# The first shift and scale with the modulation matrix as the stationary operand, for all eight output tiles

## The chip, the cores and the metric

The kernel runs on one core of a Trainium2 chip. The metric is the device time of one execution in microseconds (us); the median of three runs of the kernel before is 1396.38 us, the runs lie between 1396.1 and 1402.08. The engines are named as in the profile: PE multiplies matrices, PEld is PE's loading of the stationary operand, DVE, ACT and POOL work on vectors, SP and ACT issue the transfers (DMA).

## The reference

Two transformer blocks on a sequence of 256 tokens (stream x) beside a context of 256 tokens (stream ctx), model width 1024. What matters here is the beginning of the first layer: a modulation vector is made for each stream from its condition vector, and the first two of its six parts shift and scale the normalised activations ahead of the first projection.

```python
sc, scc = jax.nn.silu(c), jax.nn.silu(c_ctx)
mod   = jnp.split(sc  @ w_mod[l] + b_mod[l], 6, axis=-1)   # shift1, scale1, gate1, ...
mod_c = jnp.split(scc @ w_mod[l] + b_mod[l], 6)
hn = rms_norm(h, g_norm1[l]) * (1 + mod_c[1]) + mod_c[0]
xn = rms_norm(x, g_norm1[l]) * (1 + scale1) + shift1
pc, p = hn @ w_in[l], xn @ w_in[l]
```

After that come attention, a Fourier mixer, a convolution and a pooling mixer on slices of p, the output projection and a gated feed-forward, for two layers, and then a second block of the same kind. All of it is float32.

## The kernel before

Activations lie with the features on the 128 partitions: XC holds 8 tiles (k = 0 to 7) of 128 features by 512 columns, 256 of stream x and 256 of the context. Large products are made with three matmuls each (`mm3`, lines 273 to 275) from a rounded high part and a rest: AH and AL of the activations, wh and wl of the weights. The weights come as 512 KB halves through a ring of four raw buffers, are cast to wh by ACT (line 243) and reduced to wl by DVE (line 245; the second half by POOL). SP issues the transfers in the order in which the code names them; the other engines' instructions are put in order by a scheduler when the kernel is built, and each engine then works through its own list in that order.

The first projection, p_c, takes four output tiles of `in0` and accumulates over the eight k in four PSUM banks: 12 matmuls of 512 columns for each k. Before tile k can be multiplied its scale and shift must be known: `modv[:, 0, 1, :, k]` and `modv[:, 0, 0, :, k]`, two numbers for each feature, one for each stream. They are made in two ways:

- k = 0 to 3: `scf` (silu of the two condition vectors, 128 x 2 for each of eight input tiles) is the stationary operand and 512 columns of the matrix `rawm` are the moving one (line 431, p_mod, 16 matmuls). The result has two rows; ACT copies them out (line 456), PE turns them by transposes (line 459, p_modt), DVE adds the bias and forms the scale (lines 464 and 466).
- k = 4 to 7: the function `st_tile` loads one output tile of the matrix (wms, 512 KB, with the outputs on the partitions) for the scale and one for the shift. DVE multiplies it by `scb[:, 0]` and sums along the row (line 494), POOL multiplies it by `scb[:, 1]` (line 493) and ACT sums that (line 496); DVE adds the bias (lines 499 and 501). `scb` holds the condition vectors spread over all partitions; 16 transposes (line 372, p_scb) and four copies make it at the very start.

The function `in0_k` then normalises tile k (lines 481 to 485) and issues its 12 matmuls. `rb`, the reciprocal root of the mean square spread over partitions, comes from squares (lines 309 to 315), 8 matmuls with one column (line 440, p_ss), a DVE and a POOL step (lines 298 and 299) and four transposes (line 444, p_rb). After p_c come p_q, the query projection (lines 289 to 291), and p_cv, the first taps of the convolution (line 578). `scb` is also used much later by `mod_bg`, which makes the other parts of the modulation in the background.

Of the kernel before, what the change touches and what calls it, by code (L numbers as in the profile page):

```python
# [24 lines left out]
F32 = mybir.dt.float32  # L25
F32R = mybir.dt.float32r
I32 = mybir.dt.int32
AF = mybir.ActivationFunctionType
OP = mybir.AluOpType
AX = mybir.AxisListType  # L30

D = 1024
KT = 8
# [7 lines left out]
UW = T + 2 * POOL_PAD  # L41

RAW, WB, EV, NT, PTB, PEB, WMB = 4, 4, 4, 2, 2, 2, 4
WRB, WSB, N0B = 4, 5, 2
KP = 4
XAT = (0, 1, 1, 2)
RWP, XR0 = 0, 2
NPE = 8
CVD, FOD = 0.9, 1
BG0, BG1 = 2.4, 2.0  # L50
# [104 lines left out]
def tile_kernel(ctx, tc, xin, pk_d, rows_d, lc_d, bc_d, wmod0, wmod, win, wout, wfi, wfo, wsm, win2, wproj, wout2,  # L155
                wgu, wdn, wst, pos, out, dump=None):
    nc = tc.nc
    V, S, G, PE, SP = nc.vector, nc.scalar, nc.gpsimd, nc.tensor, nc.sync
# [4 lines left out]
    cpool = ctx.enter_context(tc.tile_pool(name="cp", bufs=1))  # L163
    ring = ctx.enter_context(tc.tile_pool(name="ring", bufs=1))
    wk = ctx.enter_context(tc.tile_pool(name="wk", bufs=2))
    psum = ctx.enter_context(tc.tile_pool(name="ps", bufs=4, space=bass.MemoryType.PSUM))

    def pmm(name="pmm"):
        return psum.tile([128, 512], F32, tag="mm", name=name)

    def psm(name="psm"):
        return psum.tile([128, 512], F32, tag="sm", name=name)
# [52 lines left out]
    ld = {"lim": 10 ** 6, "dma": 0, "split": 0, "raw": {}, "hl": {}}  # L225

    def dma_to(i):
        while ld["dma"] < min(i, len(halves), ld["lim"]):
            j = ld["dma"]
            raw = ring.tile([128, 1024], F32, tag="raw", name="raw", bufs=RAW)  # L230
            SP.dma_start(raw[:, :halves[j][1]], halves[j][0])
            ld["raw"][j] = raw
            ld["dma"] += 1

    def split_to(i):
        while ld["split"] < min(i, len(halves)):
# [12 lines left out]
            dma_to(j + 1 + RAW)
# [111 lines left out]
    modv = cpool.tile([128, 2, 6, 2, KT], F32, name="modv")  # L361
    scf = cpool.tile([128, KT, 2], F32, name="scf")
    for s in range(2):
        S.activation(scf[:, :, s], P("c", 8 * s, 8), AF.Silu)
    scb = lpool.tile([128, 2, D], F32, name="scb")
    lc = lpool.tile([128, LC_W], F32, name="lc")

    for s in range(2):
        for a in range(2):
            p = psm("p_scb")  # L370
            for k in range(4):
                PE.transpose(p[:, 128 * k:128 * k + 128], scf[:, 4 * a + k, s:s + 1].to_broadcast([128, 128]), ident)
            (S.copy if a else V.tensor_copy)(scb[:, s, 512 * a:512 * a + 512], p)

    def mv(l, part, s):
        return modv[:, l, part, s]
# [39 lines left out]

    sctx = ctx.enter_context(ExitStack())
    spool = sctx.enter_context(tc.tile_pool(name="st", bufs=1))
    nj = KP // 2
    ps = [pmm("p_mod") for _ in range(nj)]  # L420
    raws = []
    for k in range(KT):
        raw = spool.tile([128, 256 * KP], F32, tag="wr", name="rawm", bufs=WRB)
        raws.append(raw)
        SP.dma_start(raw, wmod0[k])
        for i, at in enumerate(XAT):
            if at == k:
                SP.dma_start(XC[:, 2 * i:2 * i + 2], xin[:, 2 * i:2 * i + 2])
    for k in range(KT):
        for j in range(nj):  # L430
            PE.matmul(ps[j][:2], scf[:, k, :], raws[k][:, 512 * j:512 * j + 512], start=k == 0, stop=k == KT - 1)
    new_ss(True)
    for k in range(KT):
        sq_acc(k, slice(0, 512), k == 0, V)
    dma_to(2)
    ld["lim"] = 2
    p = psm("p_ss")
    for i in range(4):
        for n, ss in enumerate(ss_t["ss"]):
# [2 lines left out]
    rb = psm("p_rb")  # L442
    for i in range(4):
        PE.transpose(rb[:, 128 * i:128 * i + 128], r[:, i:i + 1].to_broadcast([128, 128]), ident)
    bm1 = cpool.tile([128, KT], F32, name="bm1")
    V.tensor_scalar(bm1, P("bmod0", 8, 8), 1.0, None, op0=OP.add)
    xr = [None] * KT
    for k in range(0, XR0, 2):
        x2 = spool.tile([128, 2, 512], F32, tag="wr", name="xr", bufs=WRB)
        for i in range(2):  # L450
            V.tensor_tensor(x2[:, i], XC[:, k + i], rb, op=OP.mult)
            xr[k + i] = x2[:, i]
    pt = psm("p_modt")
    for j in range(nj):
        row = wk.tile([128, 512], F32, tag="ev", name="row", bufs=EV)
        S.copy(row[:2], ps[j][:2])
        for b in range(4):
            o = 2 * (4 * j + b)
            PE.transpose(pt[:, o:o + 2], row[:2, 128 * b:128 * b + 128], ident[:2, :2])
    ptv = pt[:, :4 * KP].rearrange("p (a k s) -> p a k s", a=2, s=2)  # L460
    for part in (1, 0):
        for s in range(2):
            d = modv[:, 0, part, s, 0:KP]
            V.tensor_tensor(d, ptv[:, part, :, s], P("bmod0", part * 8, KP), op=OP.add)
            if part == 1:
                V.scalar_tensor_tensor(d, d, 1.0, P("g1_0", 0, KP), op0=OP.add, op1=OP.mult)
    n_ = "in0"
    ps4 = [pmm("p_c") for _ in range(4)]

    def in0_k(k):  # L470
        t = spool.tile([128, 512], F32, tag="n0", name="n0", bufs=N0B)
        if xr[k] is None and k % 2 == 0:
            x2 = spool.tile([128, 2, 512], F32, tag="wr", name="xr", bufs=WRB)
            xr[k], xr[k + 1] = x2[:, 0], x2[:, 1]
        for s in (0, 1):
            c = slice(256 * s, 256 * s + 256)
            if k < XR0:
                S.activation(t[:, c], xr[k][:, c], AF.Identity, bias=mv(0, 0, s)[:, k:k + 1],
                             scale=mv(0, 1, s)[:, k:k + 1])
            else:  # L480
                V.scalar_tensor_tensor(xr[k][:, c], XC[:, k, c], mv(0, 1, s)[:, k:k + 1], rb[:, c], op0=OP.mult,
                                       op1=OP.mult)
                S.activation(t[:, c], xr[k][:, c], AF.Identity, bias=mv(0, 0, s)[:, k:k + 1])
        S.copy(AH[:, k, 0:512], t)
        V.tensor_tensor(AL[:, k, 0:512], t, AH[:, k, 0:512].bitcast(F32), op=OP.subtract)
        for m in range(4):
            mm3(ps4[m], wk256(n_, m // 2, k, 128 * (m % 2)), act(k, slice(0, 512)), k == 0, k == KT - 1)

    def st_tile(part, k):
        w = spool.tile([128, D], F32, tag="wms", name="wms", bufs=WSB)  # L490
        SP.dma_start(w, wmod[0, 8 * part + k])
        jg = spool.tile([128, D], F32, tag="jgs", name="jgs", bufs=2)
        G.tensor_tensor(jg, w, scb[:, 1], op=OP.mult)
        V.scalar_tensor_tensor(w, w, 1.0, scb[:, 0], op0=OP.mult, op1=OP.mult,
                               accum_out=modv[:, 0, part, 0, k:k + 1])
        S.activation(jg, jg, AF.Copy, accum_out=modv[:, 0, part, 1, k:k + 1])
        d = modv[:, 0, part, :, k]
        if part == 1:
            V.tensor_scalar(d, d, bm1[:, k:k + 1], P("g1_0", k), op0=OP.add, op1=OP.mult)
        else:  # L500
            V.tensor_scalar(d, d, P("bmod0", k), None, op0=OP.add)

    split_to(2)
    for i in range(2 * (KT - KP)):
        if i == RWP:
            ld["lim"] = WB
            split_to(WB)
        st_tile(1 - i % 2, KP + i // 2)
    ld["lim"] = 10 ** 6
    SP.dma_start(rows, bass.AP(tensor=rows_d.tensor, offset=rows_d.offset, ap=[[0, 128], [1, 512]]))  # L510
    SP.dma_start(lc, lc_d)
    dma_to(WB + RAW)
    for k in range(KT):
        in0_k(k)
    sctx.close()


# [2 lines left out]
    for l in range(2):  # L520
# [4 lines left out]
        with ExitStack() as mctx:  # L525
# [319 lines left out]
            for s in streams[::-1]:  # L845
                for i in range(2):
                    p = pmm("p_q")
# [550 lines left out]
def _pack(inp):  # L1398
    inp = {k: np.asarray(v) for k, v in inp.items()}
    a = {}  # L1400
# [25 lines left out]
    rows += [inp["sgu_ln_g_2"][0], inp["sgu_ln_b_2"][0]]  # L1426
    a["rows"] = np.concatenate(rows)
    a["lc"], a["bc"] = _shape_consts()
    a["wmod0"] = inp["w_mod"][0][:, :2048].reshape(8, 128, 2, 1024)[..., :128 * KP].reshape(8, 128, 256 * KP)
    a["wmod"] = inp["w_mod"].transpose(0, 2, 1).reshape(2, 48, 128, 1024)  # L1430
    qcols = np.concatenate([h * 64 + dh for h in (0, 2, 1, 3)])
    kcols = 256 + np.concatenate([h * 64 + dh for h in (0, 1)])
# [53 lines left out]
```

## Time and profile before

| | us |
|---|---|
| median of three runs | 1396.38 |
| lowest and highest run | 1396.1, 1402.08 |
| the profiled execution | 1395.62 |
| its span, first to last instruction | 1393.4 |
| mean granted PE clock | 0.983 of full |
| p_c over, p_q begins | 74.8, 75.5 |

The profile is one execution. PE is busy 1339.7 us of the span, DVE 932.3, ACT 617.5, POOL 287.9. [...] A matmul's row has its start and a modelled end; what one costs in a row of equal ones is read from the distance of two starts. A float32 matmul that is not a transpose stands in the trace as two records (two passes), each with its own weight load, and an `mm3` matmul as one.

### The profile page before, as it was taken

Reading aid. Unit: us, or ns where it says so; the run is one execution under the profiler, and the core shown is the slowest. Engines: PE = TensorE matmul, PEld = TensorE weight load, DVE = VectorE, ACT = ScalarE, POOL = GpSimd, SP = SyncE. Lnnn points to the kernel's source line nnn. Section 1 sums busy time; section 2 is a strip of 40 time slices with the busy share of each in tenths; the row PEclk is TensorE's granted clock in tenths of the full one; section 3 lists DMA queues with packets and bytes.
Section 4 is the critical chain, followed back from the end, with each engine's and each line's share of the span. In section 5 each row is a group of like instructions: output and inputs, shape, how many; then the busy total and the mean of one; then the engine's idle time right before and its main releaser. Section 6 shows DMA issues by size and latency. Waiting matters only on the chain.

```text
span 1393.4 us, 23072 instructions
## 1 busy us (share of the span) xinstructions
PE 1339.7 (96%) x9000; PEld 1193.2 (86%) x9000; DVE 932.3 (67%) x1597; ACT 617.5 (44%) x1030; POOL 287.9 (21%) x302
## 2 busy tenths in 40 slices
PE   6799889999999999999899999999999999999997
PEld 2578558888888888889689999999899999999997
DVE  4969999899885333349757666666665567755553
ACT  5623452523214232334555554455665444544452
POOL 3524535233340000121520000120100002322211
PEclk9799989999999999999999999999999999999998
DMA  8322443477895222343225555665325335555463
GB/s 321 136 92 79 166 154 134 152 272 232 278 323 179 91 91 63 104 137 107 78 83 189 183 182 156 187 242 191 122 98 175 122 125 179 181 182 181 153 196 106
DMA packets 66477, 223.77 MB, mean 161 GB/s; under 512 B 7488, under 2 KB 8640, under 8 KB 66368
## 3 DMA queue, kind: packets, MB, share of 16 engines
q1 hardware_dynamic: 53824, 178.16, 38.3%
q10 hardware_dynamic: 12080, 42.50, 9.0%
q0 software_dynamic: 464, 1.64, 0.3%
q8 instruction: 70, 1.15, 0.3%
q14 instruction: 39, 0.32, 0.1%
HBM read 221.22 MB, written 1.05 MB: 160 GB/s over the span
## 4 chain that ended last, share of the span: by engine, by line
PE 84%; DVE 9%; issue 2%; DMA 2%; POOL 1%; ACT 1%; SPq 0%; DVEq 0%; POOLq 0%; ACTq 0%
PE p_dn L273 6%; PE p_dn L275 6%; PE p_dn L274 6%; PE p_ua L273 4%; PE p_ua L274 4%; PE p_ug L273 4%; PE p_ug L275 4%; PE p_ug L274 4%; PE p_ua L275 4%; DVE wm L404 2%; DVE jg L402 2%; PE p_bq L289 2%; PE p_bq L290 2%; PE p_bq L291 2%; PE p_ga L275 2%
## 5 line engine op out<-in xcount | busy, mean ns | idle before, releaser
L245 DVE TENSOR_TENSOR wl<-raw,wh 128x1024 fp32r<-128x1024 f32 (+2 forms) x340 | 390.5, 1151 | 277.7 <-ACT wh L243 275.7
L243 ACT CAST wh<-raw 128x1024 fp32r<-128x1024 f32 (+1 forms) x344 | 331.6, 972 | 310.0 <-PE p_ug L274 89.2
L275 PE MATMUL p_dn<-HH,wl 128*128 128x256 f32 (+1 forms) x550 | 171.9, 313 | 0.5 <-DVE wl L245 0.5
L273 PE MATMUL p_dn<-HH,wh 128*128 128x256 f32 (+1 forms) x550 | 172.0, 313 | 0.0
L274 PE MATMUL p_dn<-HL,wh 128*128 128x256 f32 (+1 forms) x550 | 171.9, 312 | 0.0
L315 POOL TENSOR_TENSOR ss<-ss,sq 128x256 f32<-128x256 f32 (+1 forms) x43 | 49.8, 1158 | 422.2 <-ACT sq L314 284.7
L273 PE MATMUL p_ug<-AH,wh 128*128 128x258 f32 (+2 forms) x368 | 121.9, 332 | 0.6 <-DVE XC L891 0.6
L273 PE MATMUL p_ua<-AH,wh 128*128 128x258 f32 (+2 forms) x368 | 122.0, 333 | 0.4 <-ACT usg L950 0.3
L275 PE MATMUL p_ug<-AH,wl 128*128 128x258 f32 (+2 forms) x368 | 122.0, 332 | 0.0
L274 PE MATMUL p_ug<-AL,wh 128*128 128x258 f32 (+2 forms) x368 | 121.9, 331 | 0.0
L274 PE MATMUL p_ua<-AL,wh 128*128 128x258 f32 (+2 forms) x368 | 121.9, 331 | 0.0
L275 PE MATMUL p_ua<-AH,wl 128*128 128x258 f32 (+2 forms) x368 | 121.7, 331 | 0.0
L275 PEld LDWEIGHTS p_dn<-HH,wl 128*128 128x128 f32 x550 | 104.4, 190 | 6.7 <-DVE wl L245 0.7
L273 PEld LDWEIGHTS p_dn<-HH,wh 128*128 128x128 f32 x550 | 104.4, 190 | 6.1 <-ACT wh L243 0.2
L274 PEld LDWEIGHTS p_dn<-HL,wh 128*128 128x128 f32 x550 | 104.4, 190 | 6.1
L404 DVE SCALAR_TENSOR_TENSOR wm<-wm,scb 128x1024 f32<-128x1024 f32 x80 | 100.9, 1265 | 11.2 <-DMA wm<-in_wmod 10.4
L273 PEld LDWEIGHTS p_ug<-AH,wh 128*128 128x128 f32 x368 | 69.3, 188 | 8.1 <-DVE XC L891 0.8
L273 PEld LDWEIGHTS p_ua<-AH,wh 128*128 128x128 f32 x368 | 69.2, 188 | 7.7 <-ACT usg L950 0.5
L274 PEld LDWEIGHTS p_ua<-AL,wh 128*128 128x128 f32 x368 | 69.4, 189 | 7.3 <-DVE AL L341 0.2
L275 PEld LDWEIGHTS p_ua<-AH,wl 128*128 128x128 f32 x368 | 69.4, 189 | 7.1
L274 PEld LDWEIGHTS p_ug<-AL,wh 128*128 128x128 f32 x368 | 69.5, 189 | 6.9
L275 PEld LDWEIGHTS p_ug<-AH,wl 128*128 128x128 f32 x368 | 69.4, 189 | 6.9
(375 smaller groups left out, 3415.5 us busy)
## 6 DMA issues: line engine op xcount, KB each, us to landing
raw<-in_wfi SPq DMA_DIRECT2D x88, 512.0 KB, 4.0
raw<-in_win SPq DMA_DIRECT2D x84, 512.0 KB, 4.0
wm<-in_wmod ACTq DMA_DIRECT2D x80, 512.0 KB, 4.4
raw<-in_wgu SPq DMA_DIRECT2D x44, 512.0 KB, 3.8
raw<-in_wout SPq DMA_DIRECT2D x24, 512.0 KB, 3.6
raw<-in_wfo SPq DMA_DIRECT2D x32, 384.0 KB, 3.1
raw<-in_wfo SPq DMA_DIRECT2D x32, 320.0 KB, 3.3
raw<-in_wdn SPq DMA_DIRECT2D x16, 384.0 KB, 3.1
```

The costliest lines, as they stand in the source:

```text
L243: S.copy(h[:, :n], raw[:, :n])
L245: (G if every and j % every == 0 else V).tensor_tensor(lo[:, :n], raw[:, :n], h[:, :n].bitcast(F32), op=OP.subtract)
L273: PE.matmul(ps, w[0], a[0], start=first, stop=False, **kw)
L274: PE.matmul(ps, w[0], a[1], start=False, stop=False, **kw)
L275: PE.matmul(ps, w[1], a[0], start=False, stop=last, **kw)
L289: PE.matmul(ps, a[0], w[0], start=k == 0, stop=False)
L290: PE.matmul(ps, a[0], w[1], start=False, stop=False)
L291: PE.matmul(ps, a[1], w[0], start=False, stop=k == KT - 1)
L315: (eng or G).tensor_tensor(ss[0][:, cs], ss[0][:, cs], sq[:, :n], op=OP.add)
L402: V.scalar_tensor_tensor(jg, w, 1.0, scb[:, 1], op0=OP.mult, op1=OP.mult, accum_out=modv[:, l, part, 1, k:k + 1])
L404: V.scalar_tensor_tensor(w, w, 1.0, scb[:, 0], op0=OP.mult, op1=OP.mult, accum_out=modv[:, l, part, 0, k:k + 1])
```

## The change

All sixteen output tiles of the matrix (scale and shift, k = 0 to 7) are loaded as wms tiles, in a new layout: the inputs on the partitions, the 128 outputs along the row. For each tile k the new function `mod_k` issues 2 x 8 matmuls with a 128 x 128 piece of wms as the stationary operand and the two columns of `scf` as the moving one; the result has the outputs on the partitions, and two DVE instructions finish it. The helpers `in0_k`, `st_tile`, the transposes p_modt and the row copies are gone, as is POOL's and ACT's part in the modulation; the normalisation uses the function `norm_k` of the later layers (tiles of 256 columns). XC is loaded ahead of the matrix. `mod_k(k + 1)` is written ahead of tile k's part of p_c. The filling of `scb` is written behind p_c.

```diff
-RAW, WB, ... = 4, 4, ...
-WRB, WSB, N0B = 4, 5, 2
-KP = 4
-XAT = (0, 1, 1, 2)
-RWP, XR0 = 0, 2
+WSB = 9
+RWP = (2, 6)
...
+    def scb_fill():
...  (the p_scb transposes and copies, unchanged)
...
+    for i in range(4):
+        SP.dma_start(XC[:, 2 * i:2 * i + 2], xin[:, 2 * i:2 * i + 2])
+    wms = {}
+    ld["lim"] = 0
     for k in range(KT):
-        raw = spool.tile([128, 256 * KP], F32, tag="wr", name="rawm", bufs=WRB)
-        raws.append(raw)
-        SP.dma_start(raw, wmod0[k])
...
-    for k in range(KT):
-        for j in range(nj):
-            PE.matmul(ps[j][:2], scf[:, k, :], raws[k][:, 512 * j:512 * j + 512], start=k == 0, stop=k == KT - 1)
+        if k in RWP:
+            ld["lim"] += 2
+            dma_to(ld["lim"])
+        for part in (1, 0):
+            wms[part, k] = spool.tile([128, D], F32, tag="wms", name="wms", bufs=WSB)
+            SP.dma_start(wms[part, k], wmod0[8 * part + k])
+    ld["lim"] = 10 ** 6
+    SP.dma_start(rows, ...)
+    SP.dma_start(lc, lc_d)
...
+    def mod_k(k):
+        p = psm("p_mod")
+        for part in (1, 0):
+            for j in range(KT):
+                PE.matmul(p[:, 2 * part:2 * part + 2], wms[part, k][:, 128 * j:128 * j + 128], scf[:, j, :],
+                          start=j == 0, stop=j == KT - 1)
+        V.tensor_scalar(modv[:, 0, 1, :, k], p[:, 2:4], bm1[:, k:k + 1], P("g1_0", k), op0=OP.add, op1=OP.mult)
+        V.tensor_scalar(modv[:, 0, 0, :, k], p[:, 0:2], P("bmod0", k), None, op0=OP.add)
...
-    pt = psm("p_modt")
...
-    def in0_k(k):
...
-    def st_tile(part, k):
-        w = spool.tile([128, D], F32, tag="wms", name="wms", bufs=WSB)
-        SP.dma_start(w, wmod[0, 8 * part + k])
-        jg = spool.tile([128, D], F32, tag="jgs", name="jgs", bufs=2)
-        G.tensor_tensor(jg, w, scb[:, 1], op=OP.mult)
-        V.scalar_tensor_tensor(w, w, 1.0, scb[:, 0], op0=OP.mult, op1=OP.mult,
-                               accum_out=modv[:, 0, part, 0, k:k + 1])
-        S.activation(jg, jg, AF.Copy, accum_out=modv[:, 0, part, 1, k:k + 1])
...
+    mod_k(0)
+    split_to(2)
     n_ = "in0"
     ps4 = [pmm("p_c") for _ in range(4)]
+    for k in range(KT):
+        if k + 1 < KT:
+            mod_k(k + 1)
+        if k == 2:
+            split_to(WB)
         for s in (0, 1):
...
+            norm_k(s, k, mv(0, 1, s), mv(0, 0, s), rb[:, 256 * s:256 * s + 256])
         for m in range(4):
             mm3(ps4[m], wk256(n_, m // 2, k, 128 * (m % 2)), act(k, slice(0, 512)), k == 0, k == KT - 1)
...
+    scb_fill()
     sctx.close()
```

PE's list at the start of the program, the kernel before: the transposes p_scb come first, p_mod has 512 moving columns, and p_ss and p_rb lie between its parts.

```order
L372 MATMUL p_scb<-ident,scf 128x128 x16
L431 MATMUL p_mod<-rawm,scf 2x512 x6
L440 MATMUL p_ss<-ones,ss 128x1
...
L431 MATMUL p_mod<-rawm,scf 2x512 x6
L444 MATMUL p_rb<-ident,rs_r 128x128 x4
L431 MATMUL p_mod<-rawm,scf 2x512 x2
L459 MATMUL p_modt<-ident,row 128x2 x8
L273 MATMUL p_c<-AH,wh 128x512 x4
L274 MATMUL p_c<-AL,wh 128x512
```

The same place of the changed kernel, where p_mod has two moving columns and each matmul listed makes two passes in the trace:

```order
L451 MATMUL p_ss<-ones,ss 128x1
L451 MATMUL p_ss<-ones,ssl 128x1
...
L455 MATMUL p_rb<-ident,rs_r 128x128 x4
L440 MATMUL p_mod<-scf,wms 128x2 x32
L271 MATMUL p_c<-AH,wh 128x512
L272 MATMUL p_c<-AL,wh 128x512
L273 MATMUL p_c<-AH,wl 128x512
...
L440 MATMUL p_mod<-scf,wms 128x2 x16
...
L372 MATMUL p_scb<-ident,scf 128x128 x12
L271 MATMUL p_c<-AH,wh 128x512
...
L372 MATMUL p_scb<-ident,scf 128x128 x4
L287 MATMUL p_q<-wh,AH 128x256
```

PE begins with p_ss, the modulation of tiles 0 and 1 stands behind p_rb, that of tile k + 2 behind tile k's part of p_c, and p_scb has moved to both sides of tile 7's part.

SP's list of transfers at the start, the kernel before (rawm and wms are the modulation matrix, raw the weights of the first projection):

```order
L425 DMA rawm<-in_wmod 128x1024
L428 DMA XC<-in_xin 128x1024
...
L428 DMA XC<-in_xin 128x1024 x2
L425 DMA rawm<-in_wmod 128x1024
L428 DMA XC<-in_xin 128x1024
L425 DMA rawm<-in_wmod 128x1024 x5
L231 DMA raw<-in_win 128x1024 x4
L491 DMA wms<-in_wmod 128x1024 x8
L510 DMA rows<-in_rows 128x512
```

The same place of the changed kernel:

```order
L420 DMA XC<-in_xin 128x1024 x4
L429 DMA wms<-in_wmod 128x1024 x4
L229 DMA raw<-in_win 128x1024 x2
L429 DMA wms<-in_wmod 128x1024 x8
L229 DMA raw<-in_win 128x1024 x2
L429 DMA wms<-in_wmod 128x1024 x4
L431 DMA rows<-in_rows 128x512
```

XC has moved ahead of the matrix; the number of 512 KB tiles is the same, 4 of XC, 16 of the matrix, 4 of weights.

## Rows read from the trace of the kernel before

**Rows 1.** The page: the chain that ended last, shares of the span.

```profile
PE 84%; DVE 9%; issue 2%; DMA 2%; POOL 1%; ACT 1%; SPq 0%; DVEq 0%; POOLq 0%; ACTq 0%
```

**Rows 2.** Stretches: us, busy us of PE, PEld, DVE, ACT, POOL, then PEclk, DMA.

```profile
0.00:30.00 30.00, 21.43 (x76) 8.47 (x76) 11.12 (x22) 16.54 (x35) 5.77 (x10) 1.00 0.91 331
30.00:75.00 45.00, 29.88 (x96) 22.02 (x96) 39.43 (x50) 23.39 (x44) 25.42 (x20) 0.77 0.45 155
```

**Rows 3.** Groups by form, 30 to 68 us, p_c's to 75: busy, mean ns, idle before.

```profile
L493 POOL TENSOR_TENSOR jgs<-wms,scb 128x1024 f32<-128x1024 f32 x8 | 24.0, 3018 | 7.4 <-ACT jgs L496 6.9 <-DMA wms<-in_wmod 0.5
L494 DVE SCALAR_TENSOR_TENSOR wms<-wms,scb 128x1024 f32<-128x1024 f32 x8 | 11.9, 1493 | 0.0
L274 PE MATMUL p_c<-AL,wh 128*128 128x512 f32 x32 | 15.9, 495 | 6.9 <-DVE AL L485 6.9
L273 PE MATMUL p_c<-AH,wh 128*128 128x512 f32 x32 | 10.7, 462 | 9.9 <-ACT AH L484 9.9
```

**Rows 4.** PE in order of time, p_c: start, duration, what, count.

```profile
69.38 0.63 PE L275 MATMUL p_c<-AH,wl 128*128 128x512 f32 x1
69.80 0.63 PE L274 MATMUL p_c<-AL,wh 128*128 128x512 f32 x1
...
74.42 0.40 PE L274 MATMUL p_c<-AL,wh 128*128 128x512 f32 x1
74.66 0.39 PE L275 MATMUL p_c<-AH,wl 128*128 128x512 f32 x1
```

**Rows 5.** The chain that ended last, in order of time: start, us, what.

```profile
4.31 9.36 DMA XC<-in_xin
```

**Rows 6.** ACT, DVE and POOL in order of time: start, duration, what, count.

```profile
3.77 4.78 ACT L570 ACTIVATE cdg<-ident,pk 128x128 f32<-128x128 f32 x16 [0.67 <-POOL pk L197]
...
11.09 3.08 DVE L315 TENSOR_TENSOR ss<-ss,sq 128x512 f32<-128x512 f32 x4 [0.31 <-ACT sq L314]
...
19.35 1.04 POOL L299 TENSOR_TENSOR rs_r<-rs_v,mhalf 128x4 f32<-128x4 f32 x1 [15.62 <-DVE rs_v L298]
```

**Rows 7.** PE in order of time: the transposes p_scb and p_rb, and p_ss.

```profile
3.14 3.65 PE L372 MATMUL p_scb<-ident,scf 128*128 128x128 f32 x16 [3.14 <-ACT scf L364]
...
17.59 0.36 PE L440 MATMUL p_ss<-ones,ss 128*128 128x1 f32 x2
...
18.70 0.36 PE L440 MATMUL p_ss<-ones,ssl 128*128 128x1 f32 x2
...
24.24 0.65 PE L444 MATMUL p_rb<-ident,rs_r 128*128 128x128 f32 x4
```

**Rows 8.** Weight loads of p_c by form, 49.0 to 54.4 us, then 41.2 to 44.3.

```profile
L274 PEld LDWEIGHTS p_c<-AL,wh 128*128 128x128 f32 x5 | 1.7, 330 | 0.5
...
L274 PEld LDWEIGHTS p_c<-AL,wh 128*128 128x128 f32 x4 | 0.8, 189 | 0.2
```

**Rows 9.** PE in order of time at 188 us: p_var with one moving column.

```profile
188.14 1.95 PE L611 MATMUL p_var<-ones,lsq 128*128 128x1 f32 x16 [0.44 <-DVE awo L737]
190.01 1.12 PE L689 MATMUL p_s<-KTt,QT 64*128 64x512 f32 x2
```

**Rows 10.** Stretches around p_var (columns as in Rows 2).

```profile
188.00:190.00 2.00, 1.86 (x16) 1.86 (x16) 2.00 (x4) 1.19 (x4) 0.65 (x1) 1.00 0.72 223
190.00:192.00 2.00, 2.00 (x7) 0.94 (x6) 2.00 (x7) 0.93 (x3) 1.02 (x2) 0.80 0.55 160
192.00:194.00 2.00, 2.00 (x11) 1.30 (x12) 2.00 (x5) 0.62 (x2) 1.63 (x2) 0.50 0.60 207
```

**Rows 11.** PE in order of time: p_c begins again after two waits.

```profile
48.65 0.79 PE L274 MATMUL p_c<-AL,wh 128*128 128x512 f32 x1 [3.19 <-DVE AL L485]
...
68.78 0.79 PE L274 MATMUL p_c<-AL,wh 128*128 128x512 f32 x1 [1.63 <-DVE AL L485]
```

**Rows 12.** The stretches in which PEclk rises after them (columns as in Rows 2).

```profile
54.00:56.00 2.00, 2.00 (x9) 1.65 (x8) 2.00 (x3) 1.97 (x4) 2.00 (x1) 0.84 1.03 388
...
70.00:72.00 2.00, 2.00 (x7) 1.58 (x6) 0.46 (x1) 0.00 (x0) 1.40 (x9) 0.57 0.26 49
```

More of the change, by code (lines that the diff above doesn't have):

```diff
@@ L366, in tile_kernel @@
     lc = lpool.tile([128, LC_W], F32, name="lc")
[L368 to L373, printed above, removed]
+    def scb_fill():
+        for s in range(2):
+            for a in range(2):
+                p = psm("p_scb")
+                for k in range(4):
+                    PE.transpose(p[:, 128 * k:128 * k + 128], scf[:, 4 * a + k, s:s + 1].to_broadcast([128, 128]), ident)
+                (S.copy if a else V.tensor_copy)(scb[:, s, 512 * a:512 * a + 512], p)
     def mv(l, part, s):
@@ L418, in tile_kernel @@
     spool = sctx.enter_context(tc.tile_pool(name="st", bufs=1))
-    nj = KP // 2
-    ps = [pmm("p_mod") for _ in range(nj)]
-    raws = []
+    for i in range(4):
+        SP.dma_start(XC[:, 2 * i:2 * i + 2], xin[:, 2 * i:2 * i + 2])
+    wms = {}
+    ld["lim"] = 0
     for k in range(KT):
-        raw = spool.tile([128, 256 * KP], F32, tag="wr", name="rawm", bufs=WRB)
-        raws.append(raw)
-        SP.dma_start(raw, wmod0[k])
-        for i, at in enumerate(XAT):
-            if at == k:
-                SP.dma_start(XC[:, 2 * i:2 * i + 2], xin[:, 2 * i:2 * i + 2])
-    for k in range(KT):
-        for j in range(nj):
-            PE.matmul(ps[j][:2], scf[:, k, :], raws[k][:, 512 * j:512 * j + 512], start=k == 0, stop=k == KT - 1)
+        if k in RWP:
[5 more added lines that the diff above has]
+    ld["lim"] = 10 ** 6
+    SP.dma_start(rows, bass.AP(tensor=rows_d.tensor, offset=rows_d.offset, ap=[[0, 128], [1, 512]]))
+    SP.dma_start(lc, lc_d)
+    bm1 = cpool.tile([128, KT], F32, name="bm1")
+    V.tensor_scalar(bm1, P("bmod0", 8, 8), 1.0, None, op0=OP.add)
+    def mod_k(k):
[6 more added lines that the diff above has]
+        V.tensor_scalar(modv[:, 0, 0, :, k], p[:, 0:2], P("bmod0", k), None, op0=OP.add)
     new_ss(True)
@@ L434, in tile_kernel @@
         sq_acc(k, slice(0, 512), k == 0, V)
-    dma_to(2)
-    ld["lim"] = 2
     p = psm("p_ss")
@@ L444, in tile_kernel @@
         PE.transpose(rb[:, 128 * i:128 * i + 128], r[:, i:i + 1].to_broadcast([128, 128]), ident)
[L445 to L452, printed above, removed]
-    pt = psm("p_modt")
@@ L454, in tile_kernel @@
[L454 to L466, printed above, removed]
+    mod_k(0)
@@ L467, in tile_kernel @@
+    split_to(2)
     n_ = "in0"
     ps4 = [pmm("p_c") for _ in range(4)]
-    def in0_k(k):
[L471 to L474, printed above, removed]
-        for s in (0, 1):
[L476 to L485, printed above, removed]
+    for k in range(KT):
[3 more added lines that the diff above has]
+            split_to(WB)
+        for s in (0, 1):
+            norm_k(s, k, mv(0, 1, s), mv(0, 0, s), rb[:, 256 * s:256 * s + 256])
@@ L486, in in0_k @@
         for m in range(4):
             mm3(ps4[m], wk256(n_, m // 2, k, 128 * (m % 2)), act(k, slice(0, 512)), k == 0, k == KT - 1)
-    def st_tile(part, k):
-        w = spool.tile([128, D], F32, tag="wms", name="wms", bufs=WSB)
-        SP.dma_start(w, wmod[0, 8 * part + k])
-        jg = spool.tile([128, D], F32, tag="jgs", name="jgs", bufs=2)
-        G.tensor_tensor(jg, w, scb[:, 1], op=OP.mult)
-        V.scalar_tensor_tensor(w, w, 1.0, scb[:, 0], op0=OP.mult, op1=OP.mult,
-                               accum_out=modv[:, 0, part, 0, k:k + 1])
-        S.activation(jg, jg, AF.Copy, accum_out=modv[:, 0, part, 1, k:k + 1])
[L497 to L514, printed above, removed]
+    scb_fill()
     sctx.close()
@@ L1428, in _pack @@
     a["lc"], a["bc"] = _shape_consts()
-    a["wmod0"] = inp["w_mod"][0][:, :2048].reshape(8, 128, 2, 1024)[..., :128 * KP].reshape(8, 128, 256 * KP)
+    a["wmod0"] = inp["w_mod"][0][:, :2048].reshape(8, 128, 16, 128).transpose(2, 1, 0, 3).reshape(16, 128, 1024)
     a["wmod"] = inp["w_mod"].transpose(0, 2, 1).reshape(2, 48, 128, 1024)
```

## The prediction

> **What bounds the kernel now.** I read the chain that ended last first: PE holds 84% of the span [rows 1]. A delay of PE at the start of the program is therefore a delay of the end, unless something behind it has slack. Then the stretches. From 30 us until p_c is over, DVE is busy 39.4 of 45 us and PE only 29.9, and the PE clock was granted at 0.77 of full on average [rows 2]. The groups by form say why: eight DVE products with the matrix (1.49 us each) and eight of POOL (3.02 us each) feed the scales of tiles 4 to 7, and p_c waits for DVE's and ACT's results 6.9 and 9.9 us in sum [rows 3]. So in this stretch DVE bounds, PE idles, and its clock drops in the idle time. The last p_c matmul begins at 74.66 us and is over at 74.9 [rows 4]. That time is what the change moves; before it nothing else leaves the stage, after it PE is the chain.
>
> **What the change takes away.** DVE's and POOL's products go, and with them p_c's 16.8 us of waiting. On PE the 32 old passes of p_mod go; they lay in the input stretch, largely beside the transfers. Bytes do not change: 24 tiles of 512 KB both times. The wms buffers hold 9 of 16 tiles, so the tenth transfer waits until tile 0's first eight matmuls are done, and the weight halves 2 and 3 and the tables are queued behind it on SP. PE needs halves 2 and 3 only for tile 4, some 35 us later by the times below, so I cost that at nothing; without that cover it would be a transfer. DVE has six instructions for each tile, two of two columns and four of 256; at no more than the 0.77 us of a 512-column addition [rows 6] each that is under 4.6 us against some 9 on PE by the terms below: hidden.
>
> **The new start.** XC now comes as the first four transfers. Its last tile landed at 13.67 as one of seven [rows 5]; four of seven from about 2 us on gives 8.7. ACT is busy with the convolution taps until 8.55 either way [rows 6]. Then eight squares of about 0.55 follow, and DVE's six additions of 0.77 [rows 6] end near 14.3, 0.8 earlier than before. Now p_ss is PE's first work. Its eight matmuls are two passes each with a 128 x 128 load and one column: starts 17.59 and 18.70 with five matmuls between them give 0.222 for a matmul, 0.111 a pass [rows 7]. That was with the clock up. At the start it is not: p_scb, PE's first work before, took 3.65/16 = 0.228 for a transpose while p_rb's four took 0.65 together [rows 7]. (PEclk shows 1.00 there; the distances contradict it.) So p_ss is taken at 0.444 for a matmul, 3.55 us, until 17.8; 1.04 for POOL's power and about 0.5 for DVE and the handing over give 19.4; four transposes at 0.228 give 20.3 us, when the modulation of tile 0 can begin.
>
> **The new PE work.** Each tile costs 16 matmuls = 32 passes, a full 128 x 128 load with two columns. No row of before has that; p_ss with one column is nearest. With the clock up: 32 x 0.111 = 3.55 us (p_var, 1.95/16 = 0.122, would give 3.9 [rows 9]). With the clock down: a load's row is 330 ns instead of 189 [rows 8], so a pass lies between 0.111 (the load's start-to-start distance untouched) and 0.111 + 0.141 = 0.252. [...] A p_c part of a tile costs 12 x 0.235 = 2.8 us with the clock up and 12 x 0.427 = 5.1 us with it down [rows 4].
>
> [...]
>
> **Which level.** This decides. At 188 us sixteen passes of p_var with one column keep PE and PEld busy 1.86 of 2 us, and p_s follows without a gap [rows 9, 10]; yet the clock goes from 1.00 to 0.80 to 0.50 in the next stretches [rows 10]. PE was not idle by its rows when the clock fell; what it had done before was load weights for single columns. The changed kernel's p_mod is of just this kind, so I expect the clock to fall behind it as behind a wait. For the rise: after p_c began again at 48.65 the stretch 54 to 56 has 0.84, which with 0.50 before and 1.00 behind puts the rise at 54.6; after 68.78 the stretch 70 to 72 has 0.57, a rise at 71.7 [rows 11, 12]. That is 5.9 and 2.9 us after p_c's first matmul, and a p_c part lasts 5.1 us with the clock down. So a p_c part runs mostly at the low level, the rise comes near its end, the following p_mod gets some of the full level and lets the clock fall again. The first two p_mod groups stand together and run wholly at the low level. I take for a p_c part 4.6 us (between 2.8 and 5.1, near the upper end for the late rise) and for the later p_mod groups 4.4 us (between 3.55 and 7.1, nearer the lower, as they follow the rise).
>
> **The sum.** 20.3 + 2 x 7.1 (tiles 0, 1) + 6 x 4.4 (tiles 2 to 7) + 8 x 4.6 (p_c) + 1.9 (twelve p_scb transposes between 0.11 and 0.228) = 99.6 us for the end of p_c, against 74.8: 24.8 later. Behind it I see little that takes this back: weights and tables are there earlier, but PE did not wait for them before. The last four transposes and a few reordered instructions in layer 1 count as nothing, with 2 us for the range. The profiled execution took 1395.6, so 1420.4; the median of the runs is 0.8 above it, so **1421 us**. With 4.1 to 5.1 for p_c and 3.8 to 5.5 for p_mod, 1412 to 1432.
>
> **Rivals.**
> *The clock stays up* from p_mod's first group on, because PE has no gap any more. From 20.3: 8 x 3.55 + 8 x 2.8 + 1.8 gives 72.9 for the end of p_c, 1.9 earlier, and 1394.5 us: not slower than before; with a start up to 6 us quicker than I have it, 1388. For it: the clock was at 0.50 after waits of 3.2 and 1.6 us [rows 11], and such waits go. Against it: p_var [rows 10]. A tile at the low level costs 3.55 + 2.3 more, so it decides the sign as long as no more than a third of a tile runs there, and keeps within 0.5% up to one and a half.
> *Loads do not slow with the clock.* All p_mod groups cost 3.55, p_c as in the forecast, and p_ss 1.8: 18.5 + 28.4 + 36.8 + 1.9 = 85.6, 10.8 later, 1407 us. For it nothing but that a load's duration isn't its distance; against it the 330 ns [rows 8].
> *The clock never rises*: once it took 5.9 us of p_c [rows 11, 12], and a p_c part is over after 5.1: 20.3 + 8 x 7.1 + 8 x 5.1 + 2.7 = 120.6, 45.8 later, 1442 us. Against it: the 2.9 us.
>
> **How the numbers follow.** Forecast 0.70, clock up 0.12, loads unslowed 0.11, never rising 0.07. The forecast is 1421. The range must leave out no more than 2 in 10: from 1403, under the second rival, to 1440, just under the last one; left out are the clock staying up (0.12), most of the last rival and 0.02 of tails. A change under 0.5% (7 us, 1389.4 to 1403.4) is about what a measurement of this kernel cannot tell from none. Slower by more: 0.70 + 0.07 + nearly all of the 0.11, together 0.86. Clock up gives 0.09 for no difference and 0.03 for faster, and the second rival's lower tail 0.01 for no difference; one hundredth is left for faster by what I don't see: 0.10 and 0.04.
>
> **What would show it.** p_ss starts 0.44 apart for each matmul and begins near 14.3; tile 0's p_mod begins near 20; the first 32 of p_mod take 14 us (7 if loads do not slow); the granted clock alternates between 0.50 and 1.00 from 30 to 100 us, about 0.65 on average (1.00 in the first rival, 0.50 in the third); PE has no gap over 1 us between p_rb and p_q, and p_q begins near 100 us. POOL's product group and DVE's line-494 group are gone, 24 and 12 us. I am wrong on the bound if p_c waits for DVE or a transfer there, and wrong on the sign if p_mod runs at 0.11 a pass throughout with the clock at 1.00.

## The result, and the profile after

| | before | after |
|---|---|---|
| median of four runs each, us | 1398.66 | 1419.51 |
| lowest and highest run | 1396.1, 1402.08 | 1412.61, 1421.19 |
| the profiled execution | 1395.62 | 1420.77 |
| mean granted PE clock | 0.983 of full | 0.974 of full |
| p_q begins | 75.51 | 98.30 |

The change makes the kernel slower: the ratio is 1.0138, with an interval of 1.0094 to 1.0182. The forecast was 1421, and slower. In the two profiled executions 25.15 us are added. Of these 22.8 stand before p_q begins; the rest of the program, from p_q's start to the end of the run, took 1420.77 - 98.30 = 1322.5 against 1395.62 - 75.51 = 1320.1.

The page of the kernel after first: busy time of each engine with its share of the span, and the chain that ended last, as shares of the span (it answers [rows 1]).

```profile
PE 1375.5 (97%) x9216; PEld 1237.9 (87%) x9216; DVE 909.9 (64%) x1593; ACT 603.3 (43%) x1004; POOL 259.7 (18%) x294
...
PE 87%; DVE 7%; issue 3%; POOL 1%; ACT 1%; DMA 0%; POOLq 0%; DVEq 0%; ACTq 0%
```

DVE lost 22.4 us of work and POOL 28.2, and PE gained 35.8: the work has gone from engines with room to the one that makes the chain. The stretches after, to be laid beside [rows 2] (us, then the busy us of PE, PEld, DVE, ACT and POOL, then PEclk and DMA). PEclk is the share of full speed that PE was granted: of 855 stretches of 0.2 us of the kernel before 593 read 1.00, the full level below, and 246 read 0.50, the low level.

```profile
30.00:75.00 45.00, 45.00 (x211) 39.99 (x212) 15.87 (x36) 8.78 (x15) 0.00 (x0) 0.76 0.47 161
...
75.00:100.00 25.00, 25.00 (x133) 21.93 (x133) 8.11 (x17) 5.84 (x10) 2.92 (x12) 0.76 0.23 71
```

DVE has fallen from 39.4 to 15.9 of the 45 us and PE has no gap at all, yet the stage is longer and PEclk is no higher than before, 0.76 against 0.77. In truth it is lower: the record reads 1.00 up to its first rise, near 39.3 us, while the distances until then (0.21 us a p_mod pass, 0.43 a p_c matmul) are those of the low level (with the clock up e2 has 0.106 and 0.23). With those 9.3 us counted at 0.50 the mean from 30 to 75 us is about 0.66. The groups by form of PE from 20 to 98 us (busy, mean ns, idle before and its releaser) show that nothing else is waited for; p_rb's 2.9 us lie before the stage:

```profile
L440 PE MATMUL p_mod<-scf,wms 128*128 128x2 f32 x256 | 38.5, 286 | 0.0
L271 PE MATMUL p_c<-AH,wh 128*128 128x512 f32 x32 | 19.4, 607 | 0.0
...
L455 PE MATMUL p_rb<-ident,rs_r 128*128 128x128 f32 x4 | 1.1, 434 | 2.9 <-POOL rs_r L297 2.9
```

PE in order of time (start, duration, what, count), the first matmul of each part only:

```profile
14.26 0.59 PE L451 MATMUL p_ss<-ones,ss 128*128 128x1 f32 x2 [14.26 <-DVE ss L313]
...
20.76 1.11 PE L455 MATMUL p_rb<-ident,rs_r 128*128 128x128 f32 x4 [2.93 <-POOL rs_r L297]
21.67 13.65 PE L440 MATMUL p_mod<-scf,wms 128*128 128x2 f32 x64
35.18 0.77 PE L271 MATMUL p_c<-AH,wh 128*128 128x512 f32 x1
...
39.94 4.26 PE L440 MATMUL p_mod<-scf,wms 128*128 128x2 f32 x32
44.07 0.77 PE L271 MATMUL p_c<-AH,wh 128*128 128x512 f32 x1
...
49.33 3.74 PE L440 MATMUL p_mod<-scf,wms 128*128 128x2 f32 x32
52.94 0.75 PE L271 MATMUL p_c<-AH,wh 128*128 128x512 f32 x1
...
57.38 4.60 PE L440 MATMUL p_mod<-scf,wms 128*128 128x2 f32 x32
...
98.30 0.36 PE L287 MATMUL p_q<-wh,AH 128*128 128x256 f32 x1
```

The 64 passes of tiles 0 and 1 take 13.51 us from start to start, 0.21 each. After that a p_c part and a p_mod group take turns, 4.76 and 4.13, 5.26 and 3.61, 4.44 and 4.46, and so on, and the clock goes with them. These are stretches across one p_c part, the p_mod group behind it and the beginning of the next p_c part (columns as above; PEclk is the third number from the right):

```profile
42.00:44.00 2.00, 2.00 (x15) 2.00 (x14) 0.00 (x0) 0.00 (x0) 0.00 (x0) 0.68 0.60 178
44.00:46.00 2.00, 2.00 (x6) 1.61 (x7) 1.57 (x5) 0.91 (x2) 0.00 (x0) 0.50 0.58 184
48.00:50.00 2.00, 2.00 (x10) 1.65 (x8) 0.00 (x0) 0.00 (x0) 0.00 (x0) 0.61 0.00 0
50.00:52.00 2.00, 2.00 (x20) 2.00 (x19) 0.00 (x0) 0.00 (x0) 0.00 (x0) 1.00 0.00 0
52.00:54.00 2.00, 2.00 (x13) 1.81 (x13) 0.88 (x4) 0.05 (x1) 0.00 (x0) 0.74 0.83 262
54.00:56.00 2.00, 2.00 (x6) 1.58 (x5) 1.19 (x3) 0.86 (x2) 0.00 (x0) 0.50 0.84 146
```

PE is 2.00 of 2.00 us busy in every one of them. The p_c part from 44.07 to 49.33 runs at the low level (44 to 46); the clock rises about where it ends (48 to 50), stays up through the p_mod group (50 to 52) and falls near that group's end (52 to 54), so that the next p_c part begins at the low level again (54 to 56).

### The profile page after: what moved, and what is told of

It is laid out like the page before. It is cut to its first block, busy times and chain, and to the rows that moved or that the text cites. A ratio compares the mean times of both kernels' runs of the same rounds, so it can differ in the third digit from the quotient of the medians.

```text
span 1419.1 us, 23440 instructions
## 1 busy us (share of the span) xinstructions
PE 1375.5 (97%) x9216; PEld 1237.9 (87%) x9216; DVE 909.9 (64%) x1593; ACT 603.3 (43%) x1004; POOL 259.7 (18%) x294
## 4 chain that ended last, share of the span: by engine, by line
PE 87%; DVE 7%; issue 3%; POOL 1%; ACT 1%; DMA 0%; POOLq 0%; DVEq 0%; ACTq 0%
PE p_dn L273 6%; PE p_dn L271 6%; PE p_dn L272 5%; PE p_ua L271 4%; PE p_ua L272 4%; PE p_ug L271 4%; PE p_ug L273 4%; PE p_ug L272 4%; PE p_ua L273 4%; PE p_mod L440 3%; DVE wm L404 2%; PE p_bq L287 2%; PE p_bq L288 2%; PE p_bq L289 2%; PE p_ga L273 2%
```

## The experiments

The median of the kernel before was 1400.61 in the runs beside e1 to e4 and 1397.5 in those beside e5 to e7; single runs of one kernel lie up to 8 us from their median. "The start of p_q" is taken from the profiled execution of each, one for each kernel.

### e1: the other operand stationary

```diff
-        p = psm("p_mod")
+        q = psm("p_modr")
         for part in (1, 0):
             for j in range(KT):
-                PE.matmul(p[:, 2 * part:2 * part + 2], wms[part, k][:, 128 * j:128 * j + 128], scf[:, j, :], ...)
+                PE.matmul(q[:2, 128 * part:128 * part + 128], scf[:, j, :], wms[part, k][:, 128 * j:128 * j + 128], ...)
...
+        S.copy(row[:2, :256], q[:2, :256])
+        p = psm("p_mod")
+        for part in (1, 0):
+            PE.transpose(p[:, 2 * part:2 * part + 2], row[:2, 128 * part:128 * part + 128], ident[:2, :2])
```

> The operands of p_mod change roles and nothing else: the two columns of scf are the stationary operand and 128 outputs of wms the moving one; ACT copies the two rows out and two small transposes for each tile turn them. The number of passes is the same, 32 for each tile. Theory (the clock): passes with 128 moving columns keep the clock where p_c's passes keep it, so after a start at the low level p_mod and p_c run at the full level: p_c parts 2.8 us, p_mod groups 3.4 to 3.7 us, granted clock near 1.00 from about 30 us on, p_c over near 78 us instead of 98, 1400 us (1396 to 1406). Rival (the work): what costs is 256 passes more on PE, whichever operand moves; p_c over near 98 us or later for the added copies and transposes, 1418 to 1424 us, p_c parts still 4.6 us on average.

Measured: median 1406.32, ratio to before 1.0055 (1.0031 to 1.0079), and p_q began at 82.84 in a run of 1405.16. PE in order of time, then the stretch of [rows 2]:

```profile
27.05 3.66 PE L440 MATMUL p_modr<-wms,scf 128*2 128x128 f32 x32
...
49.19 3.66 PE L440 MATMUL p_modr<-wms,scf 128*2 128x128 f32 x32
52.77 1.20 PE L271 MATMUL p_c<-AH,wh 128*128 128x512 f32 x4
...
82.84 0.39 PE L287 MATMUL p_q<-wh,AH 128*128 128x256 f32 x1 [0.46 <-ACT sg L595]
```

```profile
30.00:75.00 45.00, 43.34 (x289) 31.15 (x287) 17.07 (x40) 11.84 (x23) 1.14 (x8) 1.00 0.45 154
```

The matrix, the tiles and the number of passes are those of the kernel after; which operand is loaded and which one streams is exchanged, with a row copy and two transposes for each tile on top, and the order is nearly the same (two of the eight groups are split by p_c matmuls). PEclk goes from 0.76 to 1.00, and 15.5 of the 22.8 us come back. The distances agree: a group such as that at 49.19, which is not split, takes 3.58 us to the next start, and four p_c matmuls behind it are over in 1.20 us. So here the low level (0.76 against 1.00 from 30 to 75 us) goes with the shape of the matmuls, not with the number of passes and not with a wait. Whether it is the load of 128 columns or the stream of two is not separated, since e1 changes both. What remains, 7.3 us, was not taken apart; in it are the first 32 passes (from 21.90 on, still partly slow: 4.50 us against 3.66), 2.0 us of waits of p_c for ACT's AH, and the PE work itself. The expectation (p_c over near 78 us, 1400 us) was missed by about 4 us: p_c was over at 82.2.

### e2: more work in the middle of each p_mod group

```diff
         for part in (1, 0):
+            if part == 0 and k > 1:
+                fz = psm("p_fill")
+                for _ in range(2):
+                    PE.matmul(fz, ident, XC[:, 0, :], start=True, stop=True)
+                V.tensor_copy(snap, fz[:, 0:1])
             for j in range(KT):
```

> The changed kernel with work added: in the middle of each p_mod group from tile 2 on stand two more float32 matmuls of 512 columns (four passes, 1.7 us at the full level, 10.2 us in all), whose result is thrown away. Theory (the clock): the added work keeps the clock up between two p_c parts, so p_mod passes take 0.11 us and p_c parts 2.8 us from tile 1 on; p_c over near 92 us instead of 98, the time 3 to 8 us shorter than the changed kernel's although 10 us of work are added, 1413 us. Rival (the work): 10 us are added, p_c over near 108 us, 1430 us.

Measured: median 1417.33, ratio 1.0119 (1.0078 to 1.0159), and p_q began at 93.77 in a run of 1418.17. PE in order of time around the first two filled groups, and the stretch:

```profile
40.45 1.84 PE L445 MATMUL p_mod<-scf,wms 128*128 128x2 f32 x16
42.15 1.96 PE L442 MATMUL p_fill<-XC,ident 128*128 128x512 f32 x4
43.95 1.84 PE L445 MATMUL p_mod<-scf,wms 128*128 128x2 f32 x16
45.65 0.47 PE L271 MATMUL p_c<-AH,wh 128*128 128x512 f32 x1
...
48.53 1.85 PE L445 MATMUL p_mod<-scf,wms 128*128 128x2 f32 x16
...
93.77 0.38 PE L287 MATMUL p_q<-wh,AH 128*128 128x256 f32 x1 [0.17 <-ACT sg L595]
```

```profile
30.00:75.00 45.00, 45.00 (x248) 37.72 (x248) 16.47 (x40) 8.77 (x15) 0.00 (x0) 1.00 0.46 163
```

The fill takes 43.95 - 42.15 = 1.80 us in a group, 10.8 in six, and computes nothing that is used. Still p_q begins 4.5 us earlier than in the kernel after, though its first p_c matmul comes at the same time (35.23 against 35.18). The clock rises at the end of the first p_c part (0.43 us between its matmuls, 0.38 for the last), and the record has 1.00 from 30 to 75 us: the next p_c part, from 45.65 to 48.53, takes 2.88 us where that of the kernel after takes 5.26. So 15.3 us of slow work were bought back. The same row gives the price of a p_mod pass with the clock up: 16 passes in 1.70 us, 0.106 each, half of the 0.21 of tiles 0 and 1. The whole profiled run is quicker than that of the kernel after by 2.6 us only (3 to 8 had been expected), which is within the scatter of single runs, and the intervals of the two ratios overlap; the clock and p_q's start carry the verdict here. What is clear of the scatter is that the run did not become 10.8 us longer.

### e3: p_mod nearly taken away

```diff
-            for j in range(KT):
+            nj = KT if k == 0 else 1
+            for j in range(nj):
...
```

> From tile 1 on only the first of the eight input tiles is multiplied (2 matmuls instead of 16 for each tile, all transfers stay), so scales and shifts are incomplete and the output is not the reference's. It shows what p_mod costs in all and whether a transfer or DVE lies hidden behind it. Theory (the clock): 28 us of p_mod go and p_c parts fall from 4.6 to 2.8 us once the first has brought the clock up: p_c over near 57 us, 1379 us. Rival (the work): p_c parts stay near 4.6 us and only the p_mod groups go: p_c over near 68 us, 1390 us. Third possibility (hidden bound): PE waits for DVE or for a wms transfer in this stage, p_c over later than 60 us with gaps of PE over 1 us.

This kernel leaves out seven of the eight input tiles from tile 1 on, so its output is not the reference's.

Measured: 1379.49 in one run, p_q at 59.60. The stretch of [rows 2] and p_q:

```profile
30.00:75.00 45.00, 44.83 (x191) 33.00 (x191) 29.83 (x61) 15.76 (x27) 2.92 (x12) 1.00 0.62 224
```

```profile
59.60 0.39 PE L287 MATMUL p_q<-wh,AH 128*128 128x256 f32 x1 [0.17 <-ACT sg L591]
```

All transfers and the DVE work are there (what is left of p_mod for tiles 1 to 4 stands with tile 0's ahead of p_c), and PE runs through with almost no gap and p_q begins 38.7 us earlier. So no transfer and no DVE bound is hidden behind p_mod down to 59.60 us: the stage after the change is as long as its PE work.

### e4: p_mod made twice

```diff
-        for part in (1, 0):
+        for part in (1, 0, 1, 0):
```

> Each p_mod group is made twice, with the same result: 256 passes more. Theory (the clock): what is added runs almost wholly at the low level, 0.21 us a pass: 13.4 us for tiles 0 and 1 and about 6.5 us for each of the others, 52 us, 1471 us; a p_mod group of tiles 2 to 7 takes about 10.5 us. Rival (the work, at the mean price of the changed kernel, 4 us for a group): 37 us, 1456 us. Rival (a pass costs 0.11 us): 28 us, 1448 us.

Measured: 1474.51 in one run, p_q at 152.03. PE in order of time, and a stretch:

```profile
53.95 10.53 PE L440 MATMUL p_mod<-scf,wms 128*128 128x2 f32 x64
...
152.03 0.36 PE L287 MATMUL p_q<-wh,AH 128*128 128x256 f32 x1
```

```profile
75.00:98.00 23.00, 23.00 (x106) 21.36 (x106) 3.99 (x12) 1.82 (x4) 0.00 (x0) 0.57 0.40 160
```

p_q moves by 53.7 us and the run by 53.7. The groups of 64 passes take 10.39, 11.00, 10.39, 11.34, 10.68 and 10.40 from their start to that of the p_c part behind them. With half as many passes such a group took 4.0 in the mean, which is close to the full level's 3.4 (2 x 1.70 in e2); the second half costs 6.7 in the mean, 0.21 a pass: in these six groups the clock, once fallen, stayed down to the group's end. PEclk is 0.57 from 75 to 98 us.

### e5: swapped, and the first two groups in PE's idle time at the start

```diff
+    scb_fill()
...
+    mod_k(0)
     p = psm("p_ss")
...
+    mod_k(1)
     rb = psm("p_rb")
...
-    mod_k(0)
...
-        if k + 1 < KT:
+        if 1 < k + 1 < KT:
             mod_k(k + 1)
...
-    scb_fill()
     sctx.close()
```

with `mod_k` as in e1.

> The swapped operands of the first experiment, and three pieces moved into PE's idle start: the filling of scb stands first again, tile 0's p_mod ahead of p_ss, tile 1's between p_ss and p_rb, where PE waited 3 us for POOL. Theory (the clock, and a stage bound by PE): tile 0's p_mod runs from about 12 us on as soon as its transfers are there, the first p_c matmul comes near 25 us instead of 31, 2 us of p_scb leave the path; p_q begins near 72 us, 1392 us (1388 to 1397), faster than before. Rival (the start is bound by the transfers or by ACT and DVE): p_c begins no earlier than 29 us, p_q not before 78 us, 1399 us.

Measured: median 1399.63, ratio 1.0011 (0.9988 to 1.0035), p_q at 78.86 in a run of 1401.3. PE in order of time, then stretches:

```profile
12.12 5.80 PE L442 MATMUL p_modr<-wms,scf 128*2 128x128 f32 x32 [5.38 <-DMA wms<-in_wmod]
...
18.71 0.38 PE L459 MATMUL p_ss<-ones,ss 128*128 128x1 f32 x2
...
21.10 6.42 PE L442 MATMUL p_modr<-wms,scf 128*2 128x128 f32 x32
...
28.18 0.65 PE L464 MATMUL p_rb<-ident,rs_r 128*128 128x128 f32 x4
```

```profile
12.00:14.00 2.00, 1.88 (x10) 1.14 (x11) 1.57 (x3) 1.75 (x4) 0.00 (x0) 0.50 1.02 412
...
18.00:20.00 2.00, 1.50 (x14) 1.49 (x14) 1.54 (x3) 1.46 (x3) 0.46 (x1) 0.99 1.03 422
20.00:22.00 2.00, 2.00 (x11) 1.64 (x12) 0.16 (x1) 0.00 (x0) 2.00 (x2) 0.50 1.04 422
```

The groups begin where they were expected, but at the low level: 5.80 and 6.42 us instead of the 3.66 of e1. Tile 0's runs after a wait of 5.38 us; the clock rises near its end (0.86 from 16 to 18 us, after 0.50), and p_ss behind it is at the upper level (0.24, later 0.22 a matmul). Then, after PE's short waits and p_ss's sixteen one-column passes, the clock falls at 20 us, and tile 1's group is slow from its first pass to near its end. So p_rb comes at 28.18 instead of e1's 20.85, and of the 10.8 us that the filled gaps were to give only 4.0 arrive. The expected start of p_q, 72, was missed by 7; the low level of the two groups makes up (5.80 - 3.66) + (6.42 - 3.66) = 4.9 of it.

### e6 and e7: the last tiles on DVE, POOL and ACT again

e6 is e5 with tiles 6 and 7 made as the kernel before makes its tiles 4 to 7; e7 does that with tiles 5, 6 and 7.

```diff
+KS = (6, 7)
+ST_AT = {1: ((1, 6),), 2: ((0, 6),), 3: ((1, 7),), 4: ((0, 7),)}
...
-        if 1 < k + 1 < KT:
+        if 1 < k + 1 < KT and k + 1 not in KS:
             mod_k(k + 1)
...
+        for part, kk in ST_AT.get(k, ()):
+            st_k(part, kk)
```

(`st_k` holds the products and sums of `st_tile` and its two DVE finishing steps; in e7 `KS` is (5, 6, 7) and tile 5's steps stand at k = 0 and 1.)

> As the fifth, with tiles 6 and 7 made as in the kernel before (DVE, POOL and ACT on rows of the matrix) while PE makes tiles 0 to 5: 6.8 us less on PE, 4 DVE products of about 1.2 us and 4 of POOL's of 3 us more, beside PE's work. Theory (PE bounds the stage, DVE has room): p_q near 65 us, 1385 us. Rival (DVE or POOL bounds again as before): PE waits over 3 us for scales of tiles 6 and 7, p_q not before 70 us, 1391 us or later.

> As the sixth, with tiles 5, 6 and 7 on DVE, POOL and ACT. Theory: another 3.4 us off PE, p_q near 62 us, 1382 us, if DVE (some 2.5 us for a tile of its own and 7 us for the products) still keeps ahead. Rival: POOL's six products of 3 us, one behind the other from the landing of tile 5 at about 30 us, are over near 50 us, and tile 7 waits: p_q near 66 us or later, 1386 us, no better than the sixth.

Measured: e6 median 1399.02, ratio 1.0011 (0.9994 to 1.0029), p_q at 73.19; e7 median 1398.62, ratio 0.9997 (0.9978 to 1.0015), p_q at 75.34. The waits of p_c in e6, then in e7, from 25 to 75 us (us in total, times, longest; e6 has 0.9 us for DVE's AL besides), and e7's stretch:

```profile
PE p_c L273 <- ACT AH L340: 3.2, 2, 1.8
...
PE p_c L274 <- DVE AL L341: 8.7, 2, 7.9
```

```profile
25.00:50.00 25.00, 17.04 (x101) 12.23 (x100) 24.35 (x27) 9.60 (x18) 17.32 (x6) 0.85 0.78 287
```

With three tiles on DVE the old bound is back: DVE is busy 24.35 of 25 us and p_c waits for it. With two tiles p_q begins 2.3 us earlier than before the change, and the median is not lower than that of the kernel before. Both expectations (p_q at 65 and 62) were missed, by 8 and 13 us. For e7 the DVE wait of 8.7 us is the largest part. In e6 p_c's first matmul came at 31.09, where e5's expectation, on which this one was built, had 25; that is most of its miss, and behind it PE waited 4.1 us for ACT and DVE. No kernel here that computes the whole result is measurably quicker than the one before.

The start differs between these executions. PE's list up to p_rb is the same in e5, e6 and e7, yet tile 1's group, behind p_ss, took 6.42, 5.32 and 3.65 us, and p_rb began at 28.18, 26.92 and 24.56. PE in order of time, e6 first, then e7:

```profile
20.94 5.32 PE L444 MATMUL p_modr<-wms,scf 128*2 128x128 f32 x32
...
31.09 1.20 PE L273 MATMUL p_c<-AH,wh 128*128 128x512 f32 x4
...
20.25 3.65 PE L444 MATMUL p_modr<-wms,scf 128*2 128x128 f32 x32
```

In e7 the clock did not fall behind p_ss (3.65 us for the group behind it, as in e1), so what e5 shows there is one outcome of several. What decides it is not shown.

### The rest of the program

The run's time less the start of p_q is 1320.1 before, 1322.5 after, and 1322.3, 1324.4, 1319.9, 1322.5, 1322.4, 1323.4 and 1321.1 in e1 to e7: within 2.5 us of 1322 while p_q's start moves over 92 us. In these runs a delay of the first stage is a delay of the end, one for one, as [rows 1] made one expect. What the few us around 1322 hang on, also the 2.4 between before and after, was not isolated. The traces show one thing that goes with it: added up from stretches of 10 us behind p_q's start (the end of the run apart), PE was at the low level for 20 us before and 34 after.

## Why the prediction was right, step by step

**The bound.** It said that p_c's end is what the change moves and that PE then has no other thing to wait for. Right: DVE and POOL gave their wait back, the groups after show 0.0 of idle time for p_mod and p_c, and e3 shows that with p_mod cut down nothing else takes its place.

**The start.** p_ss began at 14.26 (predicted 14.3) with 0.43 between matmuls (0.444). Then tile 0's p_mod came at 21.67 instead of 20.3. The step that failed is the 0.5 us "for DVE and the handing over". All engines in order of time:

```profile
17.27 0.57 PE L451 MATMUL p_ss<-ones,ssl 128*128 128x1 f32 x2
18.29 1.23 DVE L243 TENSOR_TENSOR wl<-raw,wh 128x1024 fp32r<-128x1024 f32 x1 [4.08 <-ACT wh L241]
...
19.43 0.15 DVE L296 TENSOR_SCALAR rs_v<-p_ss 128x4 f32<-128x4 f32 x1
19.66 1.04 POOL L297 TENSOR_TENSOR rs_r<-rs_v,mhalf 128x4 f32<-128x4 f32 x1 [16.03 <-DVE rs_v L296]
```

p_ss is over at 17.8, but rs_v stands behind the weight rest wl on DVE's list, DVE sat idle 4.08 us for ACT's wh, and rs_v began at 19.43. The row ahead of an instruction on its own engine had been left out of the sum.

**A pass, and the level.** Tiles 0 and 1 took 13.51 us for 64 passes, 0.211 each, and with the clock up e2 has 0.106 (predicted 0.111). No run shows the 7.1 us that the sum has for a tile's p_mod at the low level: they were the author's estimate, 0.222 a pass between the bounds of 0.111 and 0.252, half of what was taken for a p_ss matmul; the kernel after showed 13.51 / 2 = 6.76 in their place. So a pass took twice as long at the lower level, 0.211 against 0.106, as the 330 against 189 ns [rows 8] had suggested, and the second rival (loads that do not slow) is out.

**Which level where.** The clock fell near the end of p_mod and rose near the end of p_c, as read from p_var and from p_c's restarts [rows 9 to 12]; worked out from stretches of 2 us, the falls lie from 2.0 us before the end of a group to 0.4 behind it, the rises from 1.0 us before the end of a p_c part to 0.9 behind it. The reading of p_var was weaker evidence than it looked, and that it led to the right level was in part luck: the stretch ahead of [rows 10], in the kernel before, has PE busy only 0.90 of 2 us, so waits stood beside the one-column passes there.

```profile
186.00:188.00 2.00, 0.90 (x5) 0.42 (x4) 2.00 (x5) 1.21 (x4) 0.00 (x0) 1.00 0.59 195
```

That the fall needs no wait is shown by the kernel after (PE busy 2.00 of 2 us and 0.68 from 42 to 44 us), and that it goes with the shape of the matmuls by e1 (1.00 from 30 to 75 us). Later p_mod groups took 4.13, 3.61, 4.46, 3.80, 3.94 and 4.13, in the mean 4.0 (predicted 4.4, between 3.55 and 7.1). The p_c parts took 4.76, 5.26, 4.44, 5.05, 5.26, 4.44, 5.27 and, for the last one with p_scb's transposes ahead of it, 2.89, in the mean 4.67 (4.6). That the granted clock alternates was right. Its mean from 30 to 100 us was to be about 0.65; the record has 0.76, and about 0.69 with the first 9.3 us counted at the low level that their distances show. The first rival, a clock that stays up because PE has no gap, is refuted: PE has no gap from 30 to 75 us and PEclk is 0.76; e1, busy 43.34 of these 45 us, has 1.00. The third, that it never rises, is refuted by the rises (0.50 from 44 to 46 us, 1.00 from 50 to 52).

**The sum.** Predicted 20.3 + 14.2 + 26.4 + 36.8 + 1.9 = 99.6; measured 21.67 + 13.51 + 24.07 + 37.37 + 1.33 = 97.95 for the end of p_c. The differences are 1.4, -0.7, -2.3, 0.6 and -0.6: the four large terms are off by less than a tenth, and they partly cancel. The last four transposes add the 0.35 to p_q's start. Against this the rest of the program took 2.4 us more than before, for which the prediction had nothing and 2 us in its range; with it the profiled run came to 1420.77, where 1420.4 stood. That these agree within 0.4 us is luck: the terms are off by up to 2.3 us and cancel, the four runs of the kernel after lie between 1412.61 and 1421.19, and between the two medians there are 20.9 us, not 25. The lower end that the prediction gives for 4.1 and 3.8 us, 1412, should read 1413 by its own terms; nothing hangs on it.

**What the clock costs here.** With the p_mod of e2 (2 x 1.70 for a group) and p_c at its full price (2.8 us), tiles 0 and 1 would be 6.7 us shorter, the six later groups 3.7 and the p_c parts 37.37 - 22.4 = 15.0: p_q would begin at 98.30 - 25.4 = 72.9, somewhat before the 75.51 of the kernel before. This is worked out, not run. It says that the new PE work alone would about pay for the DVE waits that it removes; the 25 us of slow clock decide the sign (if nothing else then bounds the stage, for which e3 speaks), and most of that is paid by p_c, which the change did not touch.

## What to carry to other kernels

When small matrix-vector work is moved to PE, try first the form with the small operand stationary and the matrix streaming, even where that needs a row copy and transposes afterwards: here e1 against the kernel after was worth 15.5 us in the start of p_q at the same number of passes. Price such a change by the granted clock of the stretch and charge the neighbours too, since here the untouched p_c paid more for the clock than the new work itself (15.0 against 6.7 + 3.7 = 10.4 us by the reckoning above). Before filling an idle gap of PE, ask at which level it will run there: in the gaps of e5 to e7 five of six groups cost 1.4 to 1.75 times their usual 3.66 us, the sixth no more than that, and all stood ahead of what had been on time.

## What the runs showed of the hardware that was not expected

- **The recorded level at the start of the kernel after can't be taken as it stands.** The stretch below (columns as above) has PEclk 1.00, where 0.211 a pass shows the low level; the first stretch of 2 us in which the record of this kernel is below 1.00 is 42 to 44 us, after the speed has risen once, near 39.3.
- **More work, less time.** In e2 10.8 us of multiplications that nobody uses went with a stage that was 4.5 us shorter, in one execution of each kernel.
- **Here a PE without any gap held the clock worse than one with gaps.** After: 45.00 of 45 us busy at 0.76 as recorded (about 0.66 by the distances). e1: 43.34 of 45 at 1.00.
- **p_ss, too, was once followed by a fall**, as p_var is in [rows 10]: in e5 sixteen one-column passes from 18.71 on, and 0.50 from 20 us. PE had also been idle for short times just before, so this one place doesn't tell the two apart, and in e7 the same passes were followed by none.

```profile
24.00:28.00 4.00, 4.00 (x21) 4.00 (x20) 0.00 (x0) 0.00 (x0) 0.00 (x0) 1.00 0.42 135
```
